# Streaming a unit's 512 columns through TensorE in six different orders, with four offsets of the stationary tiles

## The chip, the core and the metric

The kernel runs on one core of a Trainium2 chip, so no other core shares its work. The metric is the device time of one launch in microseconds. The kernel before takes 2626.91 us (median of two runs, 2626.77 and 2627.06 us).

## The reference

Two decoder layers over 256 tokens of width 2048, everything in float32. Layer 0 mixes tokens by multi-scale retention (8 heads, chunks of 128), layer 1 by sliding-window attention (32 query heads, 4 key heads, a sink per head). Each layer goes on with a SwiGLU of hidden width 5632 and a sigmoid-gated embedding, and a last norm ends it:

```python
for i in range(DEPTH):
    h = rmsnorm(x, norm_mix[i])
    if i % N_MIXERS == 0:
        x = x + retention_mixer(h, ret_w_in[j], ret_gn[j], ret_w_out[j])
    else:
        x = x + swa_mixer(h, swa_w_in[j], swa_sinks[j], swa_w_out[j])
    x = x + swiglu(rmsnorm(x, norm_ffn[i]), ffn_w_in[i], ffn_w_out[i])
    gate = jax.nn.sigmoid(rmsnorm(x, norm_ple[i]) @ ple_w_gate[i])
    x = x + gate * (p[i] @ ple_w_proj[i])
return rmsnorm(x, norm_final)
```

Nearly all arithmetic lies in the products of the 256 rows of activations with some 495 MB of weights that are read once.

## The kernel before

**Numbers in two parts.** Each float32 operand is split into a part `hi` rounded to float32r and a rest `lo`. A product is the sum of three float32r matmuls: hi by hi (L161), lo of the weights by hi of the activations (L162), and hi of the weights by lo of the activations (L163). ScalarE makes `hi` (L211) and VectorE `lo` (L212).

**Units.** A weight matrix is cut into units of 2 x 128 rows (`KU = 2`) by 512 columns (`NW`). A unit is one DMA of 1 MB in two halves (`raw`), one split into `hi` and `lo`, and 12 matmuls: 2 row blocks `j`, 2 blocks `t` of 128 tokens, 3 products. In a matmul the activations are the stationary operand, 128 x 128 of a tile such as `xTh`, and the weights are streamed, 128 x 512 of `hi` or `lo`, into a bank of PSUM (`acc`) that holds 512 float32 columns:

```python
nc.tensor.matmul(ch.acc[n], xh, hi[:, j, cols], start=first, stop=False)
nc.tensor.matmul(ch.acc[n], xh, lo[:, j, cols], start=False, stop=False)
nc.tensor.matmul(ch.acc[n], xl, hi[:, j, cols], start=False, stop=last)
```

So each matmul has a new load of the stationary tile on TensorE, also where two in a row use the same one. The units of one output block of 512 columns form a chunk: 8 units where the inputs are the 2048 columns of the residual, 16 after retention, 22 in the second half of the SwiGLU.

**Stationary tiles.** `xTh`/`xTl` serve the products from the residual, `yTh`/`yTl` those after retention, `hTh`/`hTl` those after the SwiGLU's gate, `oTh`/`oTl` those after attention and `pTh`/`pTl` the embedding. In the built program each of them, and each `hi` and `lo` tile of weights, begins 160 bytes behind a multiple of 256 bytes in its partition.

**Order of work.** `run` walks over the units of all stages. For each it issues the load of the unit five ahead, the split of the unit three ahead, the 12 matmuls of its own, and then one step of what is pending at the side (transposes of finished blocks, scores, norms). No scheduler reorders that: each engine runs its instructions in the order in which the code issues them. In the last chunk of all, `run` lets the units go by piece of columns (512, and twice 256) rather than together, so that the end of one piece can overlap the next.

Of the kernel before, what the change touches and what calls it, by code (L numbers as in the profile page):

```python
# [11 lines left out]
F32 = mybir.dt.float32  # L12
# [6 lines left out]
P = 128  # L19
# [6 lines left out]
NW = 512  # L26
# [12 lines left out]
STEP = 4  # L39
LOADS = 5  # L40
AHEAD = 3


class Lhs:
# [6 lines left out]
    hi = property(lambda self: self.tiles[0])  # L51
    lo = property(lambda self: self.tiles[1])
# [35 lines left out]
def tile_trunk(ctx, tc, ins, out):  # L88
    nc = tc.nc
# [23 lines left out]
    def step_side():  # L113
        for g in list(side):
            try:
                next(g)
            except StopIteration:
                side.remove(g)

    def need(lhs, kts):  # L120
        n = 0
        while not all(k in lhs.ready for k in kts):
            assert side and n < 100
            step_side()
            n += 1

    def load(u, pieces=1):
        raw = wraw.tile([P, KU, NW], F32, name="raw")
        n = KU // pieces
        u.parts = [slice(j, j + n) for j in range(0, KU, n)]  # L130
        for part in u.parts:
            nc.sync.dma_start(raw[:, part, :], u.src[:, part, :])
        u.w = raw

    def split_weights(u):
        raw = u.w
        hi = whi.tile([P, KU, NW], F32R, name="hi")
        lo = wlo.tile([P, KU, NW], F32R, name="lo")
        for part in u.parts:
            split(hi[:, part, :], lo[:, part, :], raw[:, part, :])  # L140
        u.w = (hi, lo)

    def multiply(u, which, left):


        ch = u.chunk
        need(u.lhs, u.kts)
        if ch.acc is None:
            ch.acc = []
            for n, (_, cols) in enumerate(ch.pieces):  # L150
                bank, name = (ps_acc, "acc") if n < NT else (ps_at, "at")
                ch.acc.append(bank.tile([P, NW], F32, name=name)[:, : cols.stop - cols.start])
        hi, lo = u.w
        for j, k in enumerate(u.kts):
            first = not ch.begun and j == 0
            last = left == 0 and j == KU - 1
            for n in which:
                t, cols = ch.pieces[n]
                sl = slice(t * P, (t + 1) * P)
                xh, xl = u.lhs.hi[:, k, sl], u.lhs.lo[:, k, sl]  # L160
                nc.tensor.matmul(ch.acc[n], xh, hi[:, j, cols], start=first, stop=False)  # L161
                nc.tensor.matmul(ch.acc[n], xh, lo[:, j, cols], start=False, stop=False)  # L162
                nc.tensor.matmul(ch.acc[n], xl, hi[:, j, cols], start=False, stop=last)  # L163

    def run(stages, begin):


        units = [(st, u) for st in stages for u in st.units]
        for n, (_, u) in enumerate(units[:LOADS]):
            if n < AHEAD:  # L170
                next(begin)
            load(u, 1 if n else KU)
            if n < AHEAD:
                split_weights(u)
        side.append(begin)
        now = None
        pools = ExitStack()
        last = [u for _, u in units[-AHEAD - 1 :]]
        assert len({id(u.chunk) for u in last}) == 1
        for i, (st, u) in enumerate(units):  # L180

            if st is not now and (now or i >= KD // KU - AHEAD):
                pools.close()
                st.open_(st, pools)
                now = st
            if i + LOADS < len(units):
                load(units[i + LOADS][1])
            if i + AHEAD < len(units):
                split_weights(units[i + AHEAD][1])
            if u is last[0]:  # L190
                break
            ch = u.chunk
            ch.left -= 1
            multiply(u, range(len(ch.pieces)), ch.left)
            ch.begun = True
            if ch.left == 0:
                g = ch.done(ch.acc)
                if g is not None:
                    side.append(g)
            step_side()  # L200
        ch = last[0].chunk
        for n, (t, cols) in enumerate(ch.pieces):
            for i, u in enumerate(last):
                multiply(u, [n], len(last) - 1 - i)
            ch.done(ch.acc[n], t, cols)
        pools.close()
# [74 lines left out]
    def residual(stage, norm, c):  # L281


        def done(acc):
            for t in range(NT):
                xc = xs[:, t, c * NW : (c + 1) * NW]
                nc.vector.tensor_tensor(xc, xc, acc[t], op=ALU.add)
            norm.chunk(c)

            def later():  # L290
                xt = turned.tile([P, 4, S], F32, name="xt")
                yield from transposes(xt, xs[:, :, c * NW : (c + 1) * NW])
                yield from norm.places(c, xt)

            return later()

        return done


    def retention(norm, next_norm, w_in, w_out):  # L300
        yl = Lhs()

        def opened(st, pools):
            st.pool = pools.enter_context(tc.tile_pool(name="ret", bufs=2, reuse_waits="tile"))
            yl.tiles = [st.pool.tile([P, RET_OUT_K, S], F32R, name=n, bufs=1) for n in ("yTh", "yTl")]

        stage = Stage(opened)

        def head(h):
# [90 lines left out]
    def swa(norm, next_norm, w_in, w_out):  # L400
        ol = Lhs()
        st = {}

        def opened(stage, pools):
            sp = stage.pool = pools.enter_context(tc.tile_pool(name="swa", bufs=1, reuse_waits="tile"))
            ol.tiles = [sp.tile([P, KD, S], F32R, name=n) for n in ("oTh", "oTl")]
            st["rel"] = rel = sp.tile([P, 3 * P], F32, name="rel")
            nc.sync.dma_start(rel, ins["rel"])
            st["sink"] = sink = sp.tile([P, SH], F32, name="sink")
            nc.sync.dma_start(sink, ins["sinks"].to_broadcast([P, SH]))  # L410

        stage = Stage(opened)

        def kv_done(acc):
# [139 lines left out]
        n = KD // KU  # L554
        first = [Chunk(stage, residual(stage, next_norm, c)) for c in range(2)]
# [8 lines left out]
    def ffn(layer, norm, next_norm):  # L564
        hl = Lhs()

        def opened(stage, pools):
            fp = stage.pool = pools.enter_context(tc.tile_pool(name="ffn", bufs=1, reuse_waits="tile"))
            hl.tiles = [fp.tile([P, FF_K, S], F32R, name=n) for n in ("hTh", "hTl")]
            pt = turned.tile([P, 4, S], F32, name="xt")[:, 0:PLE_K, :]  # L570
            nc.sync.dma_start(pt, ins["pT"][layer])

            def later():
                for _ in range(3):
                    yield
                split(*pT, pt)

            side.append(later())

        stage = Stage(opened)  # L580

        def pair(j):
            st = []

            def gate_done(acc):
                h = stage.pool.tile([P, NT, NW], F32, name="h")
                for t in range(NT):
                    nc.scalar.activation(h[:, t, :], acc[t], AF.Silu, scale=norm.inv[:, t : t + 1])
                st.append(h)

            def up_done(acc):
                h = st[0]
                for t in range(NT):
                    nc.vector.scalar_tensor_tensor(
                        out=h[:, t, :],
                        in0=acc[t],
                        scalar=norm.inv[:, t : t + 1],
                        in1=h[:, t, :],
                        op0=ALU.mult,
                        op1=ALU.mult,  # L600
                    )

                def later():
                    hT = turned.tile([P, 4, S], F32, name="xt")
                    yield from transposes(hT, h)
                    for i in range(0, 4, 2):
                        yield
                        ks = slice(4 * j + i, 4 * j + i + 2)
                        split(hl.hi[:, ks, :], hl.lo[:, ks, :], hT[:, i : i + 2, :])
                        hl.ready.update(range(ks.start, ks.stop))  # L610

                return later()

            stage.linear(ins["ffn_w_in"][layer], j, norm.lhs, gate_done)
            stage.linear(ins["ffn_w_in"][layer], FF // NW + j, norm.lhs, up_done)

        for j in range(FF // NW):
            pair(j)
        for c in range(4):
            stage.linear(ins["ffn_w_out"][layer], c, hl, residual(stage, next_norm, c))  # L620
        return stage
# [131 lines left out]
    def load_x():  # L753
# [8 lines left out]
        for b in range(KD // KU):  # L762
# [21 lines left out]
            yield  # L784

    run(stages, load_x())


# [72 lines left out]
```

## Time and profile before

| | |
|---|---|
| median of two runs | 2626.91 us |
| the profiled execution | 2627.09 us |
| its span from the first to the last instruction | 2624.9 us |
| TensorE matmul busy | 2609.6 us, 11643 matmuls |
| stationary loads busy | 2142.0 us, 11643 loads |
| VectorE busy | 1816.8 us |
| ScalarE busy | 1221.1 us |
| read from HBM | 493.63 MB, 189 GB/s over the span |

PE is the matmul and PEld the load of its stationary tile. A matmul's row shows its duration from start to a modelled end (0.39 us for 512 columns), which is longer than the time from its start to the next matmul's start. In a timeline the first column is the start in us, and the differences of that column are the rate that counts. A row of the view by windows gives the busy time and the number of instructions of each engine in a stretch of the span.

### The profile page before, as it was taken

The numbers are of one execution on the slowest core, as the hardware profiler recorded it, in microseconds if no ns is written. First come the engines' busy times: TensorE is split into PE (matmuls) and PEld (weight loads), VectorE is DVE, ScalarE is ACT, GpSimd is POOL, SyncE is SP. The second block draws the span as 40 slices with busy tenths as digits, with TensorE's granted clock in tenths as the row PEclk, the third lists the DMA queues.
The fourth block names the chain that finished last, engine by engine and source line by source line (L and its number), as shares of the span: only waits on it lengthen the run. The fifth ranks groups of instructions, "written<-read, shape, count | busy, mean of one in ns | idle before, by whom it ended". The sixth has DMA issues, their size and how long they took to land.

```text
span 2624.9 us, 31299 instructions
## 1 busy us (share of the span) xinstructions
PE 2609.6 (99%) x11643; PEld 2142.0 (82%) x11643; DVE 1816.8 (69%) x2569; ACT 1221.1 (47%) x1525; POOL 15.1 (1%) x31
## 2 busy tenths in 40 slices
PE   9999999999999999999999999999999999999998
PEld 7888888888888888888888887777888888888887
DVE  7777777766666667676555886888757575755565
ACT  6444444444444444444444555555444444444444
POOL 0000000000000000000000000000000000000000
PEclk9999999999999999999999999999999999999999
DMA  8655555566666666666666665446665666666664
GB/s 287 186 185 188 185 189 179 183 189 188 202 190 197 192 195 191 196 189 200 192 193 194 191 197 161 127 131 204 188 198 190 197 190 198 191 195 194 193 209 143
DMA packets 139481, 497.79 MB, mean 190 GB/s; under 512 B 15808, under 2 KB 16960, under 8 KB 139200
## 3 DMA queue, kind: packets, MB, share of 16 engines
q1 hardware_dynamic: 138752, 495.20, 60.5%
q8 instruction: 91, 1.49, 0.2%
q10 hardware_dynamic: 576, 0.59, 0.1%
q14 instruction: 62, 0.51, 0.1%
HBM read 493.63 MB, written 2.10 MB: 189 GB/s over the span
## 4 chain that ended last, share of the span: by engine, by line
PE 95%; DVE 3%; issue 1%; DMA 0%; ACT 0%; SPq 0%; POOLq 0%; POOL 0%; DVEq 0%; ACTq 0%
PE acc L161 31%; PE acc L163 31%; PE acc L162 31%; DVE xt L236 1%; DVE lo L212 1%; PE at L457 1%; PE tr L509 0%; PE at L535 0%; PE at L326 0%; DMA raw<-in_ret_w_in 0%; DVE xTl L215 0%; PE at L353 0%; PE at L355 0%; PE at L354 0%; PE tr L224 0%
## 5 line engine op out<-in xcount | busy, mean ns | idle before, releaser
L212 DVE TENSOR_TENSOR lo<-raw,hi 128x1024 fp32r<-128x1024 f32 (+1 forms) x929 | 1130.8, 1220 | 698.5 <-ACT hi L211 691.0
L211 ACT ACTIVATE hi<-raw 128x1024 fp32r<-128x1024 f32 (+1 forms) x929 | 981.0, 1058 | 1186.4 <-PE acc L163 1082.9
L161 PE MATMUL acc<-hi,xTh 128*128 128x512 f32 x2592 | 1009.8, 390 | 1.5 <-ACT hi L211 0.9
L162 PE MATMUL acc<-lo,xTh 128*128 128x512 f32 x2592 | 1008.0, 389 | 0.7 <-DVE lo L212 0.7
L163 PE MATMUL acc<-hi,xTl 128*128 128x512 f32 x2592 | 1007.5, 389 | 0.6 <-DVE xTl L215 0.6
L161 PEld LDWEIGHTS acc<-hi,xTh 128*128 128x128 f32 x2592 | 486.5, 188 | 106.5 <-issue 3.9
L163 PEld LDWEIGHTS acc<-hi,xTl 128*128 128x128 f32 x2592 | 486.6, 188 | 102.5 <-DVE xTl L215 1.5
L162 PEld LDWEIGHTS acc<-lo,xTh 128*128 128x128 f32 x2592 | 486.7, 188 | 102.0 <-DVE lo L212 1.9
L161 PE MATMUL acc<-hi,hTh 128*128 128x512 f32 x704 | 273.9, 389 | 0.0
L162 PE MATMUL acc<-lo,hTh 128*128 128x512 f32 x704 | 273.9, 389 | 0.0
L163 PE MATMUL acc<-hi,hTl 128*128 128x512 f32 x704 | 273.9, 389 | 0.0
L236 DVE STREAM_TRANSPOSE xt<-h 32x256 f32<-32x256 f32 x352 | 153.5, 436 | 6.8
L163 PEld LDWEIGHTS acc<-hi,hTl 128*128 128x128 f32 x704 | 132.2, 188 | 27.6
L161 PEld LDWEIGHTS acc<-hi,hTh 128*128 128x128 f32 x704 | 132.2, 188 | 27.4
L162 PEld LDWEIGHTS acc<-lo,hTh 128*128 128x128 f32 x704 | 132.2, 188 | 27.3
L236 DVE STREAM_TRANSPOSE xt<-xs 32x256 f32<-32x256 f32 x320 | 139.6, 436 | 5.9
L161 PE MATMUL acc<-hi,yTh 128*128 128x512 f32 x256 | 99.6, 389 | 0.0
L162 PE MATMUL acc<-lo,yTh 128*128 128x512 f32 x256 | 99.6, 389 | 0.0
L163 PE MATMUL acc<-hi,yTl 128*128 128x512 f32 x256 | 99.6, 389 | 0.0
L214 ACT ACTIVATE xTh<-xt,gains 128x256 fp32r<-128x256 f32 x80 | 35.7, 499 | 60.8 <-DVE xt L236 56.3
L236 DVE STREAM_TRANSPOSE xt<-qk 32x256 f32<-32x256 f32 x128 | 55.8, 436 | 9.8 <-ACT qk L318 7.8
L236 DVE STREAM_TRANSPOSE xt<-y 32x256 f32<-32x256 f32 x128 | 55.8, 436 | 2.5
(127 smaller groups left out, 1174.2 us busy)
## 6 DMA issues: line engine op xcount, KB each, us to landing
raw<-in_ffn_w_in SPq DMA_DIRECT2D x352, 512.0 KB, 4.2
raw<-in_ret_w_in SPq DMA_DIRECT2D x191, 512.0 KB, 3.7
raw<-in_ffn_w_out SPq DMA_DIRECT2D x176, 512.0 KB, 4.2
raw<-in_ret_w_out SPq DMA_DIRECT2D x64, 512.0 KB, 3.6
raw<-in_ple_w_gate SPq DMA_DIRECT2D x64, 512.0 KB, 4.3
raw<-in_swa_w_in SPq DMA_DIRECT2D x40, 512.0 KB, 3.7
raw<-in_swa_w_out SPq DMA_DIRECT2D x32, 512.0 KB, 3.7
raw<-in_ple_w_proj SPq DMA_DIRECT2D x8, 512.0 KB, 4.2
```

Of the source, the lines that this page charges most:

```text
L161: nc.tensor.matmul(ch.acc[n], xh, hi[:, j, cols], start=first, stop=False)
L162: nc.tensor.matmul(ch.acc[n], xh, lo[:, j, cols], start=False, stop=False)
L163: nc.tensor.matmul(ch.acc[n], xl, hi[:, j, cols], start=False, stop=last)
L211: nc.scalar.activation(hi, src, AF.Copy)
L212: nc.vector.tensor_tensor(lo, src, hi.bitcast(F32), op=ALU.subtract)
L214: nc.scalar.activation(hi, src, AF.Copy, scale=scale)
L236: nc.vector.transpose(dst[b * SQ : (b + 1) * SQ, :, :, a, :], src[a * SQ : (a + 1) * SQ, :, :, b, :])
L457: nc.tensor.matmul(ats[e][:, 0:P] if b == 0 else ats[e][:, P : 3 * P], qT[sl, i, b * P : (b + 1) * P], kT[sl, j, 0 : (b + 1) * P], start=True,
```

## The change

`run` numbers the units that use one set of stationary tiles (`count`) and gives each four in a row one of six orders, over and over: the plain one, and five in which the 512 columns are taken as `n` places of the row, `run` columns from each by turns. With `(2, 16)` TensorE streams columns 0 to 15, then 256 to 271, then 16 to 31, and so on; with `(4, 16)` it goes round four places 128 columns apart. The output is addressed in the same order, so each column lands where it did. The three matmuls of a product share the order. Rows shorter than 512 columns (the pieces of 256 at the end) keep the plain one.

Three pads move stationary tiles: by 16 floats `yTh`/`yTl`, by 48 `oTh`/`oTl`, by 32 `hTh`/`hTl`. Beside the 160 bytes of before (which `xTh`/`xTl` and `pTh`/`pTl` keep) they begin at 224, 96 and 32 bytes behind a multiple of 256.

```diff
+ORDERS = [None, (2, 16), (2, 8), (2, 32), (4, 16), (2, 4)]
...
+    def streamed(cols, order):
+
+
+        if order is None or cols.shape[1] < NW:
+            return cols
+        n, run = order
+        return cols.rearrange("p (i j g) -> p j i g", i=n, g=run)
...
-                nc.tensor.matmul(ch.acc[n], xh, hi[:, j, cols], start=first, stop=False)
-                nc.tensor.matmul(ch.acc[n], xh, lo[:, j, cols], start=False, stop=False)
-                nc.tensor.matmul(ch.acc[n], xl, hi[:, j, cols], start=False, stop=last)
+                acc = streamed(ch.acc[n], u.order)
+                wh, wl = streamed(hi[:, j, cols], u.order), streamed(lo[:, j, cols], u.order)
+                nc.tensor.matmul(acc, xh, wh, start=first, stop=False)
+                nc.tensor.matmul(acc, xh, wl, start=False, stop=False)
+                nc.tensor.matmul(acc, xl, wh, start=False, stop=last)
...
+        count = {}
+        for _, u in units:
+            n = count[id(u.lhs)] = count.get(id(u.lhs), -1) + 1
+            u.order = ORDERS[n // 4 % len(ORDERS)]
...
             st.pool = pools.enter_context(tc.tile_pool(name="ret", bufs=2, reuse_waits="tile"))
+            st.pool.tile([P, 16], F32, name="pad", bufs=1)
...
             sp = stage.pool = pools.enter_context(tc.tile_pool(name="swa", bufs=1, reuse_waits="tile"))
+            sp.tile([P, 48], F32, name="pad")
...
             fp = stage.pool = pools.enter_context(tc.tile_pool(name="ffn", bufs=1, reuse_waits="tile"))
+            fp.tile([P, 32], F32, name="pad")
```

No engine has an instruction more or less, and none stands elsewhere. What differs on TensorE is the pattern of the streamed operand and of the output. At the end of the fourth unit of all (retention's first chunk) the matmuls on PE stood so, with the whole row of 512 columns in each:

```order
L161 MATMUL acc<-hi,xTh 128x512
L162 MATMUL acc<-lo,xTh 128x512
L163 MATMUL acc<-hi,xTl 128x512
L161 MATMUL acc<-hi,xTh 128x512
L162 MATMUL acc<-lo,xTh 128x512
L163 MATMUL acc<-hi,xTl 128x512
```

At the same place on PE there stands now (the lines are 11 further down in the file):

```order
L172 MATMUL acc<-hi,xTh 128x512
L173 MATMUL acc<-lo,xTh 128x512
L174 MATMUL acc<-hi,xTl 128x512
L172 MATMUL acc<-hi,xTh 128x16x2x16
L173 MATMUL acc<-lo,xTh 128x16x2x16
L174 MATMUL acc<-hi,xTl 128x16x2x16
```

From the fifth unit on, 16 rounds of 2 places of 16 columns replace the one row, in the middle of the chunk's accumulation. In the second half of the SwiGLU, where the tiles are `hTh` and `hTl`, the first step from the fifth order to the sixth reads on PE:

```order
L172 MATMUL acc<-hi,hTh 128x8x4x16
L173 MATMUL acc<-lo,hTh 128x8x4x16
L174 MATMUL acc<-hi,hTl 128x8x4x16
L172 MATMUL acc<-hi,hTh 128x64x2x4
L173 MATMUL acc<-lo,hTh 128x64x2x4
L174 MATMUL acc<-hi,hTl 128x64x2x4
```

Here 8 rounds of 4 places of 16 columns give way to 64 rounds of 2 places of 4 columns. Over the whole program the 11088 matmuls of 512 columns in L161 to L163 divide into 2136 plain ones, 2040 of `(2, 16)`, 1824 each of `(2, 8)` and `(2, 32)`, and 1632 each of `(4, 16)` and `(2, 4)`; the order changes 228 times. Of the 11088, 3264 have a stationary tile that a pad has moved.

## The prediction

> **What bounds the kernel now.** I read the busy times first.
>
> ```profile
> span 2624.9 us, 31299 instructions
> PE 2609.6 (99%) x11643; PEld 2142.0 (82%) x11643; DVE 1816.8 (69%) x2569; ACT 1221.1 (47%) x1525; POOL 15.1 (1%) x31
> PEclk9999999999999999999999999999999999999999
> PE 95%; DVE 3%; issue 1%; DMA 0%; ACT 0%; SPq 0%; POOLq 0%; POOL 0%; DVEq 0%; ACTq 0%
> PE acc L161 31%; PE acc L163 31%; PE acc L162 31%; DVE xt L236 1%; DVE lo L212 1%; PE at L457 1%; PE tr L509 0%; PE at L535 0%; PE at L326 0%; DMA raw<-in_ret_w_in 0%; DVE xTl L215 0%; PE at L353 0%; PE at L355 0%; PE at L354 0%; PE tr L224 0%
> ```
>
> TensorE is busy for 99% of the span with its clock granted in full in every slice, and the chain that ended last lies to 93% on the three lines that the change rewrites. Busy could still hide waits, so I asked next who makes TensorE wait, and what the other engines have left.
>
> ```profile
> PE acc L162 <- DVE lo L212: 2.7, 3, 1.9
> PE at L735 <- POOL sq L732: 1.3, 1, 1.3
> PE acc L161 <- ACT hi L211: 0.9, 2, 0.6
> 600.00:1300.00 700.00, 700.00 (x3089) 579.60 (x3089) 466.10 (x591) 312.28 (x343) 0.70 (x1) 1.00 0.63 194
> 1500.00:1560.00 60.00, 60.00 (x267) 49.67 (x266) 55.03 (x90) 34.53 (x51) 0.69 (x1) 1.00 0.61 189
> 1580.00:1740.00 160.00, 159.95 (x797) 116.69 (x796) 122.12 (x312) 91.02 (x218) 0.00 (x0) 1.00 0.45 138
> ```
>
> The waits sum to 5 us in the whole program. In the windows the columns are the stretch, PE, PEld, DVE, ACT, POOL, the clock, and the share and rate of the DMA. From 600 to 1300 us, where TensorE does nothing but matmuls of 512 columns, it starts 3089 in 700 us: 226.6 ns each. VectorE is busy for 67% there, 92% at the tightest place (1500 to 1560 us), and the DMA engines for 63%. So the time is the number of matmuls times the interval between their starts, and nothing else is within 8% of it.
>
> The change leaves the number alone. Everything hangs on whether the interval depends on the order in which columns are read and written, and on where the stationary tile lies. I looked for the parts of the interval. At the end of the program there are pieces of 256 columns:
>
> ```profile
> 2614.75 0.28 PE L163 MATMUL at<-hi,xTl 128*128 128x256 f32 x1
> 2614.87 0.28 PE L161 MATMUL at<-hi,xTh 128*128 128x256 f32 x1
> ...
> 2615.47 0.28 PE L163 MATMUL at<-hi,xTl 128*128 128x256 f32 x1
> ```
>
> Six intervals in 0.72 us are 120.0 ns each. 256 columns more cost 226.6 - 120.0 = 106.6 ns, 0.416 ns a column. 512 columns are then 213.2 ns, and 13.4 ns of each interval are a part that does not grow with the columns. Times 11088 this is 149 us, all that any order could win: 2627 - 149 = 2478 us.
>
> Is this part a fixed price or a contention of the two reads, stream and stationary tile? Two places speak.
>
> ```profile
> 46.77 1.02 PE L326 MATMUL at<-xt 128*128 128x256 f32 x4
> 47.63 0.61 PE L328 MATMUL at<-xt 128*128 128x128 f32 x4
> 47.99 0.48 PE L162 MATMUL acc<-lo,xTh 128*128 128x512 f32 x1
> 48.30 0.40 PE L163 MATMUL acc<-hi,xTl 128*128 128x512 f32 x1
> 48.54 0.40 PE L161 MATMUL acc<-hi,xTh 128*128 128x512 f32 x1
> 48.77 0.40 PE L162 MATMUL acc<-lo,xTh 128*128 128x512 f32 x1
> 49.01 0.39 PE L163 MATMUL acc<-hi,xTl 128*128 128x512 f32 x1
> 49.23 0.39 PE L161 MATMUL acc<-hi,xTh 128*128 128x512 f32 x1
> 49.46 0.40 PE L162 MATMUL acc<-lo,xTh 128*128 128x512 f32 x1
> ...
> 50.39 0.39 PE L163 MATMUL acc<-hi,xTl 128*128 128x512 f32 x1
> 50.62 0.39 PE L161 MATMUL acc<-hi,xTh 128*128 128x512 f32 x1
> 50.84 0.39 PE L162 MATMUL acc<-lo,xTh 128*128 128x512 f32 x1
> ```
>
> After a head's scores (L326, L328) the intervals are uneven, 0.22 to 0.24 us, and only at 50.4 us do they come back to the steady 0.23, 0.22. The nine from 48.30 to 50.39 us take 2.09 us, 232 ns each. Nothing waits there on data. So the same instruction on the same kind of operand can take 5.6 ns more, or up to 7 ns less (0.22 from 49.01 to 49.23 us at face value; the view rounds to 0.01), by how it falls in with its neighbours, and it settles into one beat. Something between consecutive matmuls and stationary loads does interact. The four plain float32 matmuls of 256 columns take 0.86 us, 215 ns each, 0.84 ns a column: half the rate. That is the one row of a slower stream that the trace has.
>
> Against an influence of addresses speaks that the beat is one and the same for all stationary tiles:
>
> ```profile
> L161 PE MATMUL acc<-hi,xTh 128*128 128x512 f32 x704 | 273.9, 389 | 0.0
> L161 PE MATMUL acc<-hi,yTh 128*128 128x512 f32 x195 | 75.9, 389 | 0.0
> L161 PE MATMUL acc<-hi,hTh 128*128 128x512 f32 x131 | 51.0, 389 | 0.0
> ```
>
> In the built program they lie up to 140 KB apart; they have the same 389 ns in a window in which VectorE and ScalarE write and read the same memory at 67% and 45%. But all of them begin 160 bytes behind a multiple of 256, as the streamed tiles do, so the trace has nothing on another offset.
>
> **The change part by part.** *Orders.* 8952 matmuls read and write in jumps. No row shows a jump. If a jump costs nothing, the term is zero. The nearest rows bound it: minus 7 ns each as in the one short interval, -63 us; plus 5.6 ns each as in the unsettled stretch, +50 us; far off, the half rate of L326 in one order, dealt with below. I take zero, since the 0.416 ns a column and the steady beat are what thousands of rows show whatever else goes on in the memory, and a run of four columns is still contiguous.
>
> [...]
>
> *Changes of order.* There are 228. Each may throw TensorE out of its beat once. The stretch above cost 2.09 us less 9 x 226.6 ns = 0.05 us, so between 0 and 228 x 0.05 = 11 us. I take half, 6 us.
>
> *Pads.* They add no instruction. 3264 matmuls have a moved stationary tile: zero if offsets don't matter, 3264 x 5.6 ns = 18 us if they never settle, -23 us at 7 ns less. I take zero with the same reason. ScalarE and VectorE write the moved tiles in steps of whole rows as before, and lie beneath TensorE in any case.
>
> *Cover.* Loads, splits and evacuations are the same instructions in the same places. A faster TensorE would meet VectorE's 92% from 1500 to 1560 us only beyond an 8% gain, and the most is 149 of 2627 us, 5.7%.
>
> Sum: 2627.1 (the profiled execution, 2.2 us above its span and 0.2 us above the median) + 0 + 6 + 0 = 2633 us.
>
> **The rivals.** *A: the beat does not care* (the forecast), 2627 to 2638 us.
>
> *B: the jumps part the two reads, and the interval falls.* For it: the constant 13.4 ns, and that it moved when the phase between stream and stationary load moved. With two places in turn the stream goes along its addresses at half the speed, and could stay clear of a stationary load that runs beside it. Against: no interval that stays below 226 ns anywhere. Price: the 7320 matmuls in two places by all of 13.4 ns, -98 us, 2529 us; by half, -49 us, 2578 us. It passes 2% (52.5 us) where those 7320 gain over 7.2 ns each.
>
> *C: the jumps keep TensorE from its beat, and the interval rises.* The place is L172 to L174 in the five new orders. For it: the stretch from 48.30 us, which shows the cost of being out of step, and that being in step is a state it has to reach. Against: it gets there after each of the interruptions by scores. Price: 8952 x 5.6 ns = +50 us, 2677 us; at 0.24 us (13.4 ns more) +120 us, 2747 us. It decides from 5.9 ns a matmul on, which is 2%.
>
> *D: the shortest runs stream at half rate.* By L326's 0.84 ns a column a matmul takes 430 ns; the 1632 of `(2, 4)` alone give 1632 x 203 ns = +331 us, 2958 us. All 8952 would give +1817 us, 4444 us. [...] For it in the trace is nothing; against it, that runs of four columns still come in neighbours.
>
> **How the numbers follow.** A has 0.50, B 0.20, C 0.21, D 0.09. Within 2% (some 52 us, about what a measurement here can tell from no change) I count A, a third of B (0.06) and 40% of C (0.08): 0.64 at first sight. But A and the small halves of B and C rest on one beat at one offset; orders and offsets mixed make a large effect of either sign likelier than a tie between them, so I move 0.06 to B's and 0.02 to C's large parts. That leaves 0.56 within, 0.20 faster, and 0.24 slower (D and the rest of C). The time is A's, 2633 us. The range drops D (0.09), the upper end of C and the lower end of B: 2550 to 2725 us.
>
> **What would show it.** By A the matmuls of all six orders have 389 ns and start 226.6 ns apart, and the count in a window of 700 us stays near 3089. By B the groups of two places are shorter, and some interval stays near 0.22 us; by C starts stay uneven at 0.23 to 0.24 us; by D one shape has double the interval and its load waits. A difference between `xTh` and `hTh` in the same order would show that the offset matters. The forecast is wrong if any one order's interval differs by over 10 ns, even if the total happens to balance.

## The result and the profile after

The changed kernel takes 2749.18 us (2748.77 and 2749.58) against 2626.91 us: a ratio of 1.0465, interval 1.0448 to 1.0483. It is 122 us slower, outside the range of 2550 to 2725 us.

The page of the changed kernel has the same instructions, the same clock (0.999), and TensorE still at the limit:

```profile
span 2746.6 us, 31299 instructions
PE 2733.6 (100%) x11643; PEld 2156.7 (79%) x11643; DVE 1822.1 (66%) x2569; ACT 1227.6 (45%) x1525; POOL 15.1 (1%) x31
PEclk9999999999999999999999999999999999999999
PE 98%; DVE 1%; issue 0%; DMA 0%; ACT 0%; SPq 0%; POOLq 0%; POOL 0%; DVEq 0%; ACTq 0%
L172 PE MATMUL acc<-hi,xTh 128*128 128x512 f32 x2592 | 1040.0, 401 | 1.7 <-ACT hi L226 1.7
```

The mean duration of a matmul rose from 389 to 401 ns, and it waits for nobody new. The view by windows (columns as before the change) has fewer starts in the same stretch:

```profile
600.00:1300.00 700.00, 700.00 (x2938) 554.89 (x2937) 444.37 (x560) 298.86 (x323) 0.70 (x1) 1.00 0.59 185
```

2938 starts against 3089: 238 ns each. The order changes every 48 matmuls, so the timeline of TensorE gives each order's interval. These are the first matmuls of seven stretches in a row, all on `xTh`: plain, (2,16), (2,8), (2,32), (4,16), (2,4), and plain again.

```profile
1180.38 0.40 PE L172 MATMUL acc<-hi,xTh 128*128 128x512 f32 x1
...
1191.28 0.40 PE L172 MATMUL acc<-hi,xTh 128*128 128x512 f32 x1
...
1202.80 0.41 PE L172 MATMUL acc<-hi,xTh 128*128 128x512 f32 x1
...
1214.48 0.40 PE L172 MATMUL acc<-hi,xTh 128*128 128x512 f32 x1
...
1225.84 0.40 PE L172 MATMUL acc<-hi,xTh 128*128 128x512 f32 x1
...
1236.94 0.41 PE L172 MATMUL acc<-hi,xTh 128*128 128x512 f32 x1
...
1248.93 0.40 PE L172 MATMUL acc<-hi,xTh 128*128 128x512 f32 x1
```

The stretches divided by 48 give 227 ns for plain, 240.0 for (2,16), 243.3 for (2,8), 236.7 for (2,32), 231.3 for (4,16) and 249.8 for (2,4). Over the whole trace, from the start of one matmul to that of the next (without the few intervals over 300 ns, at waits and interruptions):

| order | matmuls | mean interval | above the 226.8 ns of before | together |
|---|---|---|---|---|
| (2,16) | 2040 | 240.0 ns | 13.2 ns | 27 us |
| (2,8) | 1824 | 243.3 ns | 16.5 ns | 30 us |
| (2,32) | 1824 | 236.7 ns | 9.9 ns | 18 us |
| (4,16) | 1632 | 232.8 ns | 6.0 ns | 10 us |
| (2,4) | 1632 | 250.1 ns | 23.3 ns | 38 us |
| plain | 2136 | 228.9 ns | 2.1 ns | 4 us |

The sum is 127 us. The span grew by 2746.6 - 2624.9 = 121.7 us; the intervals over 300 ns, which the means leave out, went the other way, from 39.3 us in all to 32.6. The place is found; the cause is not. The orders (2,16), (2,8) and (2,32) have the same interval whichever stationary tile they use, moved or not, to within 0.2 ns. The plain order has 227.3 ns on `xT`, but 233.4 on `yT` and 232.5 on `hT`, whose tiles a pad has moved, and (4,16) has 231.5 ns on `xT` and 236 to 237 on the moved tiles. What the other engines do at the same time doesn't show: (2,16) has 240.0 ns in stretches in which VectorE is busy for 43% and in stretches in which it is busy for over 90%.

### The profile page after: what moved, and what is told of

Same layout as the page of the kernel before. It is cut to its first block, busy times and chain, and to the rows that moved or that the text cites. A ratio compares the mean times of both kernels' runs of the same rounds, so it can differ in the third digit from the quotient of the medians.

```text
span 2746.6 us, 31299 instructions
## 1 busy us (share of the span) xinstructions
PE 2733.6 (100%) x11643; PEld 2156.7 (79%) x11643; DVE 1822.1 (66%) x2569; ACT 1227.6 (45%) x1525; POOL 15.1 (1%) x31
## 4 chain that ended last, share of the span: by engine, by line
PE 98%; DVE 1%; issue 0%; DMA 0%; ACT 0%; SPq 0%; POOLq 0%; POOL 0%; DVEq 0%; ACTq 0%
PE acc L172 32%; PE acc L174 32%; PE acc L173 32%; PE at L474 1%; DVE xt L251 0%; PE at L552 0%; PE tr L526 0%; DVE lo L227 0%; PE at L342 0%; DMA raw<-in_ret_w_in 0%; PE at L371 0%; PE at L370 0%; PE at L369 0%; PE tr L239 0%; PE at L344 0%
## 5 line engine op out<-in xcount | busy, mean ns | idle before, releaser
L172 PE MATMUL acc<-hi,xTh 128*128 128x512 f32 x2592 | 1040.0, 401 | 1.7 <-ACT hi L226 1.7
L174 PE MATMUL acc<-hi,xTl 128*128 128x512 f32 x2592 | 1038.1, 400 | 0.0
L173 PE MATMUL acc<-lo,xTh 128*128 128x512 f32 x2592 | 1036.8, 400 | 0.5 <-DVE lo L227 0.5
L172 PEld LDWEIGHTS acc<-hi,xTh 128*128 128x128 f32 x2592 | 489.5, 189 | 130.1 <-issue 3.9
L173 PEld LDWEIGHTS acc<-lo,xTh 128*128 128x128 f32 x2592 | 490.1, 189 | 126.8 <-DVE lo L227 1.4
L174 PEld LDWEIGHTS acc<-hi,xTl 128*128 128x128 f32 x2592 | 489.4, 189 | 126.8 <-issue 0.7
L174 PE MATMUL acc<-hi,hTl 128*128 128x512 f32 x704 | 283.3, 402 | 0.0
L173 PE MATMUL acc<-lo,hTh 128*128 128x512 f32 x704 | 283.3, 402 | 0.0
L172 PE MATMUL acc<-hi,hTh 128*128 128x512 f32 x704 | 283.3, 402 | 0.0
L173 PEld LDWEIGHTS acc<-lo,hTh 128*128 128x128 f32 x704 | 133.3, 189 | 35.3
L172 PEld LDWEIGHTS acc<-hi,hTh 128*128 128x128 f32 x704 | 133.3, 189 | 35.3
L174 PEld LDWEIGHTS acc<-hi,hTl 128*128 128x128 f32 x704 | 133.3, 189 | 35.2
L174 PE MATMUL acc<-hi,yTl 128*128 128x512 f32 x256 | 103.3, 403 | 0.0
L172 PE MATMUL acc<-hi,yTh 128*128 128x512 f32 x256 | 103.1, 403 | 0.0
L173 PE MATMUL acc<-lo,yTh 128*128 128x512 f32 x256 | 102.9, 402 | 0.0
L173 PEld LDWEIGHTS acc<-lo,yTh 128*128 128x128 f32 x256 | 48.5, 189 | 13.1
```

The source lines that it names most:

```text
L172: nc.tensor.matmul(acc, xh, wh, start=first, stop=False)
L173: nc.tensor.matmul(acc, xh, wl, start=False, stop=False)
L174: nc.tensor.matmul(acc, xl, wh, start=False, stop=last)
```

## Experiments

At first two theories stood against each other. By **contention**, C of the prediction, the jumps make the stream run into the reads of the stationary load. By the **stream's own price**, jumping costs the read (or the write into PSUM) whatever the stationary load does.

### The two parts of the change, each alone

Orders without pads (the three pad lines are taken out again):

```diff
-            st.pool.tile([P, 16], F32, name="pad", bufs=1)
...
-            sp.tile([P, 48], F32, name="pad")
...
-            fp.tile([P, 32], F32, name="pad")
```

> The six orders without the three pads, so all stationary tiles begin 160 bytes behind a multiple of 256 again. In the changed kernel the plain order took 226.7 ns a matmul on the unmoved xT and 233 ns on yT and hT, the two-place orders the same on all tiles. If the offset matters for the plain order alone, the pads cost 384 x 5.9 ns on hT, 144 x 6.7 ns on yT, about 96 x 3 ns on oT, and some 2 us in the four-place order: about 6 us, so about 2743 us. If the offsets are what spoils the orders, it falls much further, towards 2640 us.

Measured: 2744.18 us, ratio 1.0446 (1.0429 to 1.0464). The orders make all but 5 us of the loss.

Pads without orders (the three pad lines are put into the kernel before):

```diff
+            st.pool.tile([P, 16], F32, name="pad", bufs=1)
...
+            sp.tile([P, 48], F32, name="pad")
...
+            fp.tile([P, 32], F32, name="pad")
```

> The three pads on the kernel before, all columns in the plain order. If the interval of the plain order depends on where the stationary tile begins (233.4 ns at 64 bytes off, 232.5 at 128, 229.7 at 192, against 226.7), 768 x 6.7 + 2112 x 5.9 + 384 x 3.0 ns = 19 us are added: about 2646 us. If those intervals were left over from the changes of order, it stays at 2627 us.

Measured: 2644.75 us, ratio 1.0068 (1.0053 to 1.0083): 18 us. The groups of this kernel (count, then busy us and mean ns) show where:

```profile
L162 PE MATMUL acc<-lo,xTh 128*128 128x512 f32 x2592 | 1008.9, 389 | 0.5 <-DVE lo L212 0.5
L162 PE MATMUL acc<-lo,hTh 128*128 128x512 f32 x704 | 278.0, 395 | 0.0
L162 PE MATMUL acc<-lo,yTh 128*128 128x512 f32 x256 | 101.3, 396 | 0.0
```

The unmoved `xTh` keeps its 389 ns; the moved tiles have 395 and 396. So the place of a stationary tile does matter to the plain order. The 18 us that the pads cost alone shrink to 5 us beside the orders, where only the plain rows and those of (4,16) are clearly slower with the pads, by some 3 and 2 us; (2,4) moves by up to 2.2 ns on `yT` and `oT`, and the other two-place orders keep their interval.

### Reading or writing

Seven ways in turn, each on its own line; `acc` is the output in PSUM, `w` the streamed tile:

```diff
...
+                    elif way == 4:
+                        nc.tensor.matmul(acc, x[:, k, sl], jump(w, 2, 4), start=f, stop=l)
+                    elif way == 5:
+                        nc.tensor.matmul(jump(acc, 2, 4), x[:, k, sl], w, start=f, stop=l)
+                    elif way == 6:
+                        nc.tensor.matmul(jump(acc, 2, 4), x[:, k, sl], jump(w, 2, 4), start=f, stop=l)
```

> Seven ways in turn, 22 units each, each way on its own line: plain; read in jumps of (2,16) with the output written straight; the output in jumps and the read straight; both; and the same three for (2,4). Where only one side jumps, the columns of the result are permuted. If the stream's reading is what jumps slow (alone or against the stationary load), read alone takes what both take (240 and 250 ns, a mean duration of about 403 and 415 ns in the groups, against 389) and write alone stays at 227 (389). If the writing into PSUM is what slows, it is the other way round.

The groups of this kernel: L172 reads in (2,16), L174 writes in it, L176 does both; L178, L180 and L182 are the same for (2,4).

```profile
L172 PE MATMUL acc<-hi,xTh 128*128 128x512 f32 x376 | 151.7, 403 | 0.0
L174 PE MATMUL acc<-hi,xTh 128*128 128x512 f32 x296 | 115.4, 390 | 0.0
L176 PE MATMUL acc<-hi,xTh 128*128 128x512 f32 x340 | 137.1, 403 | 0.0
L178 PE MATMUL acc<-hi,xTh 128*128 128x512 f32 x380 | 158.2, 416 | 0.0
L180 PE MATMUL acc<-lo,xTh 128*128 128x512 f32 x444 | 173.8, 391 | 0.0
L182 PE MATMUL acc<-hi,xTh 128*128 128x512 f32 x340 | 141.5, 416 | 0.0
```

Reading alone costs what both cost, 403 and 416 ns; writing alone has the plain duration. By starts the intervals are 240.0, 226.7 and 240.0 ns, and 250.0, 226.7 and 250.0 (one block of units of the write in (2,4) had 229.7). So the write into PSUM in runs of four and of sixteen columns from two places is free. No run has runs of two in the output alone.

### The stationary operand

First its addresses: 128 columns in a row, every second column, or one column 128 times, with three orders of the stream.

```diff
...
+                    elif way == 3:
+                        nc.tensor.matmul(acc, x[:, k, t : S : 2], w, start=f, stop=l)
...
+                    elif way == 6:
+                        nc.tensor.matmul(acc, same(x[:, k, t * P : t * P + 1]), w, start=f, stop=l)
...
```

> Nine ways in turn, 17 units each: three orders (plain, (2,16), (2,4)) by three ways to take the 128 stationary columns: in a row as before (512 bytes of each partition), every second column (spread over 1024 bytes, so twice the pieces of memory for the same number of columns), and one column 128 times (4 bytes). In the second the tokens are permuted, in the third all outputs of a block of tokens are of one token. If stream and stationary load contend, every second column lengthens the interval and one column shortens it, in all orders: by lines of memory the 13 ns of the plain order would become up to 27 and near zero (groups near 402 and 376 ns). If the jumps cost by themselves, all three ways of the stationary operand have the same interval in each order (389, 403, 415 ns in the groups).

The groups of the plain order with every second column (L176) and with one column (L182), which had 389 ns in the kernel before:

```profile
L176 PE MATMUL acc<-hi,xTh 128*128 128x512 f32 x232 | 91.7, 395 | 0.0
L182 PE MATMUL acc<-hi,xTh 128*128 128x512 f32 x336 | 133.2, 396 | 0.0
```

Intervals by starts, in ns, for plain, (2,16) and (2,4): in a row 226.7, 240.0, 250.0; every second column 233.4, 242.2, 256.5; one column 231.5, 240.0, 248.6. Spreading the load costs 2 to 7 ns, but drawing it together to 4 bytes does not shorten the plain interval; it lengthens it. Neither theory had that.

Then its size. With 64 columns:

```diff
...
+                    elif v == 3:
+                        nc.tensor.matmul(acc[0:64], x[:, k, half], w, start=f, stop=l)
+                    elif v == 4:
+                        nc.tensor.matmul(jump(acc[0:64], 2, 16), x[:, k, half], jump(w, 2, 16), start=f, stop=l)
...
```

> Six ways in turn, 22 units each: plain, (2,16) and (2,4) with 128 stationary columns, and the same with 64 (the first and last product of a chunk keep 128, so that every output is begun and ended; 64 of each 128 tokens lack most of their sum). If stream and stationary load contend for reads, half a load leaves half of what each interval has above 213.3 ns: 220 for plain (13.3 halved), 227 for (2,16) and 232 for (2,4). If the jumps cost the stream by themselves, the three intervals stay 13 and 23 ns apart from each other: plain somewhere from 216 to 227, (2,16) 13 ns above it, (2,4) 23 ns above it.

Plain 230.1, (2,16) 240.0, (2,4) 246.7 ns. Half the load does not halve anything. Nor do the orders keep their distances of 13 and 23 ns from plain, as they should if the jumps alone set the price: they lie 10 and 17 ns above it. With 32 columns and with one:

```diff
...
+                    elif v == 8:
+                        nc.tensor.matmul(acc[0:1], x[:, k, t * P : t * P + 1], w, start=f, stop=l)
+                    elif v == 9:
+                        nc.tensor.matmul(jump(acc[0:1], 2, 16), x[:, k, t * P : t * P + 1], jump(w, 2, 16), start=f, stop=l)
+                    elif v == 10:
+                        nc.tensor.matmul(jump(acc[0:1], 2, 4), x[:, k, t * P : t * P + 1], jump(w, 2, 4), start=f, stop=l)
...
```

> Twelve ways in turn, 13 units each: plain, (2,16), (2,4), (32,4), each with 128, 32 and 1 stationary column (the first and last product of a chunk keep 128; the others leave out the remaining tokens' sums). With one column the stationary load reads 4 bytes of a partition against the stream's 2048. If the reads of the stationary load are what lengthens the intervals, one column brings all orders to about 216 ns (the interval that bfloat16 showed in five of six orders). If the stream's own jumps from line to line cost, (2,4) stays near 250 and (2,16) near 240 ns with one column too. With half a load the plain order went up, to 230, and (2,4) down, to 247, which speaks for the stream's own price, with the load a small term of either sign.

The groups of this kernel with 128 stationary columns (L170 is (2,16), L172 is (2,4)) and with one (L184 plain, L186 (2,16), L188 (2,4)):

```profile
L170 PE MATMUL acc<-hi,xTh 128*128 128x512 f32 x274 | 110.5, 403 | 0.0
L172 PE MATMUL acc<-hi,xTh 128*128 128x512 f32 x223 | 92.6, 415 | 0.0
...
L184 PE MATMUL acc<-hi,xTh 128*1 128x512 f32 x258 | 102.1, 396 | 0.0
L186 PE MATMUL acc<-hi,xTh 128*1 128x512 f32 x244 | 98.6, 404 | 0.0
L188 PE MATMUL acc<-hi,xTh 128*1 128x512 f32 x181 | 74.7, 413 | 0.0
```

With 32 stationary columns the intervals are 231.6, 240.0 and 246.9 ns. With one, 4 bytes a partition against the stream's 2048, (2,16) keeps its 240.0 ns and (2,4) has 248.5 of 250.0. Contention with what the load reads is out as the main cause: it is the stream's own read that is slower. The load's part is a term of a few ns of either sign. The plain order even goes up to 230.8 ns with one column, so its 226.7 is not simply a price of the stream and a price of the load added up.

### The number of bytes

The split tiles `hi` and `lo` in bfloat16, two bytes a column:

```diff
...
-        hi = whi.tile([P, KU, NW], F32R, name="hi")
-        lo = wlo.tile([P, KU, NW], F32R, name="lo")
+        hi = whi.tile([P, KU, NW], BF16, name="hi")
+        lo = wlo.tile([P, KU, NW], BF16, name="lo")
...
```

> The tiles hi and lo of weights and activations in bfloat16 rather than float32r, so each column is two bytes (and the three products keep some 16 bits rather than float32r's more). Six ways in turn, 22 units each: plain, (2,32), (2,16), (2,8), (2,4), (4,16). If the read of four-byte columns at the full rate leaves too little room for the stationary load and for jumps, half the bytes give both room: all six ways near one interval between 213 and 220 ns. If the jumps or the part that does not grow with columns belong to each instruction, bfloat16 keeps the 13 ns of plain and the 13 and 23 ns that (2,16) and (2,4) add.

Groups: L167 plain, L171 (2,16), L173 (2,8), L175 (2,4).

```profile
L167 PE MATMUL acc<-hi,xTh 128*128 128x512 bf16 x572 | 216.3, 379 | 2.3 <-ACT hi L230 2.3
L171 PE MATMUL acc<-hi,xTh 128*128 128x512 bf16 x416 | 157.8, 379 | 0.0
L173 PE MATMUL acc<-hi,xTh 128*128 128x512 bf16 x272 | 103.1, 379 | 0.0
L175 PE MATMUL acc<-hi,xTh 128*128 128x512 bf16 x340 | 131.7, 387 | 0.0
```

By starts: 215.8 ns for plain, (2,32), (2,16), (2,8) and (4,16) alike (214.4 in some of the first blocks), and 226.7 ns for (2,4). So 10.9 of the 13.4 ns that the prediction found beside the columns go with float32r. A shorter stationary load is not the reason, as one column of float32r left the plain order at 230.8 ns. Runs of 16 bytes and more cost nothing at two bytes a column (215.8 ns as in plain); runs of 8 bytes cost 10.9 ns and have the 226.7 ns of plain float32r. Why was not shown: no run separates the number of bytes from the type in which TensorE multiplies. The kernel took 2529.88 us in one execution, with the (2,4) units in it, beside 2626.83 us; no run shows what the smaller parts do to the precision.

### What the jump's length does

Two kernels with more orders by turns, reading and writing in the same one. The first:

```diff
...
+                    if way == 0:
+                        nc.tensor.matmul(jump(acc, 2, 2), x[:, k, sl], jump(w, 2, 2), start=f, stop=l)
+                    elif way == 1:
+                        nc.tensor.matmul(jump(acc, 2, 64), x[:, k, sl], jump(w, 2, 64), start=f, stop=l)
...
+                    elif way == 10:
+                        nc.tensor.matmul(jump(acc, 32, 4), x[:, k, sl], jump(w, 32, 4), start=f, stop=l)
...
```

> Twelve more orders in turn, 13 units each, reading and writing in the same order: (2,2), (2,64), (2,128), (4,4), (4,8), (4,32), (4,64), (8,16), (8,32), (16,16), (32,4), (64,4). The two-place orders so far: 236.7 ns for runs of 32, 240.0 for 16, 243.3 for 8, 250.0 for 4. If jumps cost by themselves, the interval follows the number of jumps whatever the number of places: (4,32) and (8,32) equal 240 and so on, (4,4) equals (2,4) at 250. If the stationary load's reads are met or missed by where the stream goes, the number of places matters as much (the four-place order of 16 had 231.5 at the same 32 runs that cost 240 with two places), and some order may come below 226.7.

The second:

```diff
...
+                    if way == 0:
+                        nc.tensor.matmul(jump(acc, 32, 8), x[:, k, sl], jump(w, 32, 8), start=f, stop=l)
...
+                    elif way == 9:
+                        nc.tensor.matmul(jump(acc, 32, 4), x[:, k, t : S : 2], jump(w, 32, 4), start=f, stop=l)
...
```

> Eleven ways in turn, 14 units each: (32,8), (32,2), (16,4), (16,8), (8,4), (8,8), (64,2), (128,2), and (32,4) with the stationary columns in a row, every second one, and one column 128 times. So far runs of 4 columns had 250.0 ns with places 1024 bytes apart, 268 at 512, 223.7 at 64 and 233 at 32, so the step from line to line matters, not the number of jumps. [...] For the stationary side with (32,4): one column 128 times and every second column move the interval by up to 7 ns, as in the plain order.

The groups of (4,4) and (32,4) in the first kernel, and of (8,4) and (64,2) in the second:

```profile
L173 PE MATMUL acc<-hi,xTh 128*128 128x512 f32 x156 | 68.1, 437 | 0.0
L187 PE MATMUL acc<-hi,xTh 128*128 128x512 f32 x194 | 74.7, 385 | 0.0
L178 PE MATMUL acc<-hi,xTh 128*128 128x512 f32 x212 | 93.7, 442 | 0.0
L182 PE MATMUL acc<-hi,xTh 128*128 128x512 f32 x216 | 138.8, 643 | 0.0
```

All float32r orders that were run, by the length of a run and the step from one place to the next (interval in ns by starts; the plain order is 226.7; two values where blocks of units in the same order differ):

| step between places | runs of 2 (8 bytes) | 4 (16) | 8 (32) | 16 (64) | 32 (128) | 64 (256) | 128 (512) |
|---|---|---|---|---|---|---|---|
| 1024 bytes (2 places) | 333 | 250.0 | 243.3 | 240.0 | 236.7 | 226.7 | 226.7 |
| 512 (4) | | 268.0 | 231.1 | 231 to 237 | 233.3 | 226.7 | |
| 256 (8) | | 276.2 | 233 or 259 | 239.5 | 236.7 | | |
| 128 (16) | | 246.7 | 220 or 231 | 240.0 | | | |
| 64 (32) | 431 | 223.3 or 226.6 | 232.4 | | | | |
| 32 (64) | 461 | 233.3 | | | | | |
| 16 (128) | 451 | | | | | | |

The number of jumps doesn't set the price: four-column runs always jump 127 times and cost from 223.3 to 276.2 ns. Two estimates failed: from 223.7 ns at a step of 64 bytes and 268 at 512, the author put (16,4) near 224 and (8,4) at up to 268, and they have 246.7 and 276.2; runs of 8 bytes were put at the 333 of (2,2) and cost up to 461. Runs of 256 bytes are free (226.7 ns). With (32,4), every second stationary column and one column 128 times have 223.9 and 223.1 ns, within the 7 ns that were expected.

An order does not always have one interval. (32,4), 16 bytes and then a step of 64, has two repeating patterns in the starts, on the same tiles: four intervals of 218, 230, 224 and 221 ns, or seven of 221, 234, 239, 225, 226, 220 and 222. Most blocks of units keep the one into which they fall. In the second kernel, one block of seven had the first; in the kernel with few stationary columns, all six with 128 columns had it. (16,8) has 220 ns in its first block and 230.7 in all later ones, (8,8) 233 and 259. The runs don't say what decides which pattern a block takes.

### The place of the streamed tile

> All columns in the plain order, sixteen ways in turn, 10 units each: the streamed tiles hi and lo begin 0, 16, 32 ... 240 bytes further than before, so that stream and stationary tile lie apart by that much. Contention of the two reads by place in memory: the interval runs through a pattern of 226.7 ns at 0, about 233 at 192 bytes (stationary 64 further), 232 at 128, 230 at 64, and offsets between may lie lower or higher than any of these, between 216 and 243 ns. If only whether both are alike matters, all offsets but 0 have about 232 ns. If it is not the relative place but the stationary tile's own place, all sixteen stay at 226.7.

```diff
...
+            q.tile([P, KU * NW + 64], F32R, name=name)[:, 4 * u.way : 4 * u.way + KU * NW].rearrange(
+                "p (k n) -> p k n", n=NW
+            )
...
```

The kernel took 2681.8 us in one execution beside 2626.83. Two groups of this kernel, at 160 bytes (L191) and at 208 bytes (L197), beside 389 ns before:

```profile
L191 PE MATMUL acc<-hi,xTh 128*128 128x512 f32 x232 | 92.9, 401 | 0.0
L197 PE MATMUL acc<-hi,xTh 128*128 128x512 f32 x120 | 47.7, 397 | 0.0
```

By starts, the plain order has 226.7 ns at offset 0 and means from 228.4 to 234.7 ns at the fifteen others, eleven of these from 231 to 234. Offset 0, where stationary and streamed tiles begin alike modulo 256 bytes, has the lowest mean and is the only one with 226.7 ns in every block. At 240 bytes three of five blocks have 226.7 ns too, the other two 230.3 and 233.9. With the order (32,4) at the same sixteen offsets:

```diff
-                nc.tensor.matmul(ch.acc[n], xh, hi[:, j, cols], start=first, stop=False)
...
+                        nc.tensor.matmul(jump(acc, 32, 4), x[:, k, sl], jump(w, 32, 4), start=f, stop=l)
...
```

> Every unit in the order (32,4), the streamed tiles 0, 16 ... 240 bytes further on, sixteen ways of 10 units. At offset 0 this order had 218, 230, 224, 221 ns in turn, a mean of 223.7. If the relative place of stream and stationary tile matters as in the plain order (226.7 to 234.7 ns), the sixteen spread by several ns around 224 and the best may come near 216; if this order goes through all the memory's parts alike, they are all about 224 ns, and the whole kernel takes about 2627 - 11088 x 3.0 ns = 2594 us.

2621.19 us in one execution beside 2627.07. The means of the sixteen offsets spread from 220.5 to 230.8 ns, and at some of them the blocks differ: at offset 0 two blocks on `xT` have 223.3 to 223.6 ns, and five, on `xT` and `hT`, 226.2 to 226.6; at 112 bytes the first block has 243.3 and the later ones 227.3 to 227.8. At 208 bytes the interval was a steady 220.0 ns on `xT` and `hT`.

### A version that is faster

All rows in (32,4), the streamed tiles 208 bytes further on, everything else as before:

```diff
+SHIFT, PLACES, RUN = 52, 32, 4
...
-        hi = whi.tile([P, KU, NW], F32R, name="hi")
-        lo = wlo.tile([P, KU, NW], F32R, name="lo")
+        hi, lo = (
+            q.tile([P, 64 + KU * NW], F32R, name=name)[:, SHIFT : SHIFT + KU * NW].rearrange("p (k n) -> p k n", n=NW)
+            for q, name in ((whi, "hi"), (wlo, "lo"))
+        )
...
+        return cols.rearrange("p (i j g) -> p j i g", i=PLACES, g=RUN)
...
```

> The kernel before with every row of 512 columns read and written in the order (32,4), four columns (16 bytes) and then a step of 64 bytes, and with the streamed tiles 208 bytes further on in their partition, where this order had a steady 220.0 ns a matmul on xT and hT (234 ns on oT, few of them). All products are computed. If the price belongs to the stream's own steps from line to line and stays as it was in blocks of ten units, 10704 matmuls gain 6.7 ns and 384 lose 7 ns: 2627 - 72 + 3 = 2558 us, 2.6% faster than before. If the 220 ns came only by what the blocks around it left behind, the beat falls back to the mean of the sixteen offsets, 225.8 ns, and the kernel takes about 2617 us.

Measured: 2558.88 us (2558.18 to 2559.7), ratio 0.974 (0.9727 to 0.9754). Page, windows and timeline of this kernel:

```profile
span 2556.7 us, 31299 instructions
PE 2537.8 (99%) x11643; PEld 2143.1 (84%) x11643; DVE 1816.0 (71%) x2569; ACT 1215.5 (48%) x1525; POOL 15.1 (1%) x31
```

```profile
600.00:1300.00 700.00, 700.00 (x3184) 597.28 (x3183) 471.93 (x590) 320.01 (x352) 0.70 (x1) 1.00 0.65 200
```

```profile
1000.10 0.38 PE L170 MATMUL acc<-hi,xTh 128*128 128x512 f32 x1
1000.32 0.38 PE L171 MATMUL acc<-lo,xTh 128*128 128x512 f32 x1
1000.54 0.38 PE L172 MATMUL acc<-hi,xTl 128*128 128x512 f32 x1
```

3184 starts in 700 us where there were 3089: 220 ns each, on every stationary tile, `oT` too. The order of the columns, which made the change slower, makes the kernel 2.6% faster than before with this step and this offset. It takes both: at 208 bytes the plain order had 234.6 ns, and at offset 0 the order (32,4) had 223.3 or 226.6.

## Why the prediction was wrong

**What bounds the kernel** held. The time is the number of matmuls times their interval: 122 us are 127 us of longer intervals, less what the intervals over 300 ns, at waits and interruptions, became shorter. Cover, loads, splits and evacuations played no part, as said.

**The step that failed** is "Orders": "If a jump costs nothing, the term is zero ... I take zero, since the 0.416 ns a column and the steady beat are what thousands of rows show whatever else goes on in the memory, and a run of four columns is still contiguous." All those rows read columns in one order; none could show a price of another. The term measured 123 us, 6.0 to 23.3 ns a matmul. The upper bound taken from the unsettled stretch, +50 us, was no bound: it priced a matmul out of step with its neighbours and not a slower read. The range ended at 2725 us because it took in no more of C than its smaller prices.

**Changes of order**, 6 us, were no cost of that size. The first twelve matmuls behind each change together differ by less than 1 us from what their blocks settle to. (There are 233 changes in the order in which `run` issues the units, not 228.)

**Pads** at zero were wrong in the plain order (18 us alone; the part named 18 us for tiles that never settle, but they run in steady intervals of some 232 and 233 ns, so that the figures agree by chance) and small beside the orders (5 us, ratios 1.0465 and 1.0446).

**A** (0.50) fell. **B** (0.20) fell as the change was made: two places in turn raise the interval on every tile, by 9.9 to 23.3 ns. Its kernel of truth was that part of the 13.4 ns depends on how columns are read: (32,4) with the offset of 208 bytes takes 6.7 off, and bfloat16 takes 10.9 off. The lever was a step of 64 bytes and not two distant places. **C** (0.21) has the right sign and, at its upper end of 2747 us, nearly the time, but that is a coincidence, since its cause was wrong: the orders have steady beats of their own, and one stationary column leaves 240.0 and 248.5 ns of 240.0 and 250.0. **D** (0.09) named the right operand, the stream, and the right order as the worst, at a price nine times too high (23 ns in place of 203; its 430 ns a matmul do come about with runs of two columns, at 431 to 461 ns); all 8952 at that price, 4444 us, no run shows, as the other four orders have 232.8 to 243.3 ns. On the output's side there is no price to find in these orders: the write alone has 226.7 ns.

**The reading that misled** was that of the stretch behind L326 and L328. That the interval wavers there was read as contention of two reads. In the unrounded starts of the kernel before, the same series of some nine intervals, from 224 to 236 ns, follows the scores of all eight heads before the beat is back, so it is a fixed way into a beat. The 7 ns less that the prediction used as a lower bound were rounding: no interval between these matmuls is under 224 ns. The runs show something narrower than contention: the stationary tile's place and columns move the interval by up to 7 ns, the stream's own pattern by up to 235 ns (461 against 226.7). The prediction also expected a single beat, and some patterns have two, as (32,4) with 223.3 and 226.6 ns.

One more reading was off without effect: VectorE's tightest place is not the 92% from 1500 to 1560 us, as it is busy throughout from 1773 to 1778 us.

What stays open: why a step of 64 bytes is good and one of 256 bad for runs of 16 bytes (223.3 or 226.6 ns against 276.2), why the plain order is steadiest where both tiles begin alike (226.7 ns in every block), and what decides which of two patterns a block falls into. The table above shows no rule that covers it, and no run shows by what means a step sets the interval.

## What to carry to other kernels

In this kernel, which streams float32r back to back, the pattern in which the moving operand is read moved the interval from 226.7 ns to anything from 220 to 461, and the place where its tile or the stationary one begins moved the plain order's to up to 234.7. In another such kernel, try patterns and offsets by turns, each on its own line and in several blocks, and read each block's interval from the starts, since one pattern can have two intervals (223.3 and 226.6 ns for (32,4) on the same tiles). Take the price of an access pattern from a trace that has one, not from many rows of another pattern. The write into PSUM was free in both orders tried by itself, (2,16) and (2,4) (226.7 ns each), so a column order that helps the read can probably be given to the output without a price.

## What had not been expected

- One stationary column in place of 128 does not shorten any of the three intervals by more than 1.6 ns, and lengthens the plain one from 226.7 to 230.8 ns.
- Float32r in its plain order pays 10.9 ns a matmul (226.7 against 215.8) that bfloat16 doesn't. Runs of 8 bytes have 333 to 461 ns in float32r (2 columns) and 226.7 in bfloat16 (4 columns).
- A permuted read can be faster than a straight one: 220.0 ns in steps of 64 bytes against 226.7.
